# A two-layer decoder trunk on one core: where the reciprocal of the recurrence stands, how the first MLP marks its spare time, in what pieces a residual is loaded and which engine normalises

## The chip, the cores and the metric

The kernel runs on one core of a Trainium2 chip. A core has five engines that work side by side, each through its own list of instructions in order: TensorE (PE, the matrix multiplications and the transposes), VectorE (DVE, element-wise work on vectors), ScalarE (ACT, functions and casts), GpSimd (POOL) and SyncE (SP, which only issues transfers here). Transfers between the large memory and the core's own memory run on 16 DMA engines. An engine that reaches an instruction whose input is not there waits, and everything behind that instruction on the same engine waits with it.

The metric is the device time of one execution in microseconds (us). Before the change it was 2046.99 us, the median of 3 runs (2044.89 to 2050.0).

## What is computed

The trunk has two layers of width 1024 over 1024 positions, all in float32. Each layer is a mixer and an MLP, each followed by a layer norm of the scaled residual plus the branch:

```
for i in range(2):
    mix = hgrn2_mixer(x, ...)  if i == 0 else  conformer_conv_mixer(x, ...)
    x = layer_norm(ALPHA * x + mix, ...)
    ff = square(relu(x @ ffn_w1[i])) @ ffn_w2[i]        # 1024 -> 4096 -> 1024
    x = layer_norm(ALPHA * x + ff, ...)
```

The first mixer is a gated linear recurrence with 8 heads: projections of x give q, a forget gate, v and an output gate; per head a state `S` of 128 by 128 is carried along the sequence, `S_t = diag(f_t) S_{t-1} + k_t v_t^T` and `o_t = S_t^T q_t`; then a norm, a gate and an output projection. The second mixer is a convolution module: a projection to 2048 columns, a gate, a causal depthwise convolution over 31 positions, a layer norm with a sigmoid gate, and a projection back to 1024.

## The kernel before, in words

Every float32 product is made of reduced-precision products. A factor is split into a rounded high part and the rest (a cast on ACT, then a subtraction on DVE), and three matmuls take the place of one. On top of that the large products use a form with 7 instead of 8 block products, whose weight blocks are sums of blocks (`form`; `sum_pieces` and its relatives make these sums in the large memory by adding transfers). The unit of PE's work is a matmul of 128 by 128 by 512 columns, of which the kernel issues thousands in each stage.

The stages, by the time at which PE works on them in the profiled execution: the projection of v (5 to 85 us); the recurrence's heads with the other projections as filler (85 to 410); the output projection and norm (410 to 504); the first MLP's upward half (504 to 817) and downward half (817 to 1125); the first projection of the convolution in two halves of the sequence, with the convolution itself on DVE, ACT and POOL beside it (1125 to 1526); in that stretch the projection back, `second(0)` for the first half from about 1288 and `second(1)` for the other from about 1466; the second MLP (1526 to 2039). The last results leave by 2047.

Up to the end of the recurrence the order of the instructions is that in which the code was written. The heads are generators (from L700 on): each `yield` ends a step, a list of chores interleaves the steps with filler matmuls, and `later(1, ...)` defers a small job to the next step. After that a scheduler of the framework orders each engine's list by its own estimate of the times and by dependences; `keep_in_program_order` and `behind` restrict it.

What the change touches:

- **The recurrence's reciprocal.** For the part of the scores inside small blocks a head needs `kd`, on DVE the product of a cut of `B` with `rt`, the reciprocal of `totals[4]`. The reciprocal is issued one step ahead of that product (L730 to L733). `state` is the carried state: a copy and three updates, then three more updates, in two chains per head, and PE's products `state,qk` wait for them.
- **The spare work of the first MLP.** Weight blocks for the convolution's projections are split ahead of time and written back to the large memory under the names `ready`. `spare` (L1486) does one unit of it: a small DVE copy into `now` (a mark, which reads the form that PE takes next and so sets the earliest time), a cast on ACT and a subtraction on DVE of the block `next` loaded by the mark before, two stores of `ready`, and the load of the following `next`, held back by a small POOL copy that reads the mark. In the first MLP's upward half `Forms` calls it when a form is made, by the rate 3 in 8; there a POOL copy also holds back the cast (`late_cast`). In the downward half it is called 30 times. There are 38 units.
- **The gate of `sum_pieces`** (L453). The copies of a weight sum are held back by a transfer of one element, issued by SP from a form of the MLP.
- **The norm of the convolution**, `normalise`. For each half 8 pieces of 128 by 512 are scaled and shifted: 6 on ACT, 2 on DVE (the odd ones of the left columns).
- **The residual of `second(0)`**, `residual_of`. Four transfers of 512 KB bring it from `kept` into a buffer that the transposes of `finish` read before; they are issued after the last of its 8 column blocks.
- **The evictions of `second`** (from L1768). For each tile the product's result is added to the scaled residual, then a bias; for the right columns an operation named `ahead` scales the residual and adds the bias before the product is there.

Of the kernel before, what the change touches and what calls it, by code (L numbers as in the profile page):

```python
# [8 lines left out]
F32 = mybir.dt.float32  # L9
# [259 lines left out]
def body(ctx, tc, d, out):  # L269
# [24 lines left out]
    def run(kb, n, size):  # L294
        return [kb + i * size for i in range(n)]

    def slots(kbs, name):
        return ring(kbs, (2, 1024), name, F32R)

    def raws(kbs, name="raw"):  # L300
        return ring(kbs, (1024,), name)
# [153 lines left out]
    def sum_pieces(name, layer, c):  # L455

        t = sums[name, layer, c] = dram.tile([4, P, 1024], F32, name=f"sum_{name}{layer}{c}")
        v, w = t.rearrange("a p n -> p a n"), d[name][layer, c].rearrange("a p n -> p a n")

        def copy(i, q):  # L460
            def go(after):
                nc.sync.dma_start(out=t[i : i + 1, 0, 0:1], in_=after)
                nc.sync.dma_start(out=v[:, i], in_=w[:, q])

            return go

        def add(out, x, **kw):
            return lambda after: nc.gpsimd.dma_start(out=out, in_=x, accum_op=ALU.add, **kw)

        def chained(i):  # L470
            return add(v[:, i], v[:, i - 1], max_dma_last_dim=4096)

        return [copy(0, 0), copy(1, 2), add(v[:, 0:2], w[:, 2:4]), copy(2, 0), chained(2), copy(3, 1), chained(3)]
# [196 lines left out]
    def mul(o, a, b):  # L670
        vector.tensor_tensor(out=o, in0=a, in1=b, op=ALU.mult)

    def cutout(t, at, dims):
        return bass.AP(tensor=t.tensor, offset=t.offset + at, ap=[t.ap[0], *dims])
# [6 lines left out]
    def recurrence(h):  # L681
# [45 lines left out]
        yield  # L727
        rt, kd = p1("rt"), p1("kd")
        other, mine = [[n2 - 4, 2], [8, P], [1, 4]], [[n2 + 4, 2], [8, P], [1, 4]]
        vector.reciprocal(rt, totals[4])  # L730
        later(1, lambda: nc.scalar.copy(out=cutout(kd, 4, other), in_=cutout(B, 4, other)))
        yield
        mul(cutout(kd, 0, mine), cutout(B, 0, mine), cutout(rt, 0, [[1, 2], [2, P], [0, 4]]))  # L733
        scale(4)
        yield
# [747 lines left out]

    hold, staged = [], []

    def spare(after, late_cast=False):  # L1486

        if not hold:
            return
        slot, raw = hold  # L1490
        now = stat.tile([P, 2, 4], F32, tag="ss", name="ss")[:, 0, :1]
        nc.vector.tensor_copy(out=now, in_=after)
        if staged:
            key = staged.pop()
            if late_cast:
                nc.gpsimd.tensor_copy(out=slot[:, 0, :1], in_=now)
            nc.scalar.copy(out=slot[:, 0].bitcast(F32R), in_=raw)
            vector.tensor_tensor(out=slot[:, 1].bitcast(F32R), in0=raw, in1=slot[:, 0], op=ALU.subtract)
            ready[key] = tuple(dram.tile([P, 1024], F32, name=f"ready{len(ready)}_{i}") for i in range(2))
            for i in range(2):  # L1500
                nc.sync.dma_start(out=ready[key][i], in_=slot[:, i])
        if ahead:
            name, at = ahead.pop(0)
            nc.gpsimd.tensor_copy(out=raw[:, :1], in_=now)
            nc.sync.dma_start(out=raw, in_=d[name][at])
            staged.append((name, at))

    fw = Forms(nc, vector, slots((144, 152, 48, 112, 120), "fw"), raws(run(192, 4, 4)), raws(run(160, 2, 4), "sum"), lambda after: spare(after, True), 3, range(44))
    fw.todo = [[(blocks("w1q", 0, c), 2 if c < 2 else 0)] for c in range(NFC)]
    up = Up()  # L1510

# [7 lines left out]
    up.settle(0)  # L1519
    fw.ahead(3)  # L1520
    up.ws = bank((6, 7, 3, 4))
    summing = []
    for c in range(NFC):
        for i in ORDER[2 if c < 2 else 0 :]:
            (f,) = fw.take(1)
            fw.ahead(3)
            if (c, i) == (0, 7):
                bg.done()
            up.form(c, i, f)
            if summing:  # L1530
                summing.pop(0)(f[:1, 1, :1].bitcast(F32))
        if c in (0, 2):
            summing += sum_pieces(*to_sum.pop(0))
        if c == 0:
            up.settle(1)
            hold += [view(208, (2, 1024), F32, "spare"), view(216, (1024,), F32, "next")]
# [147 lines left out]
    def normalise(half):  # L1684

        for job in conv[KB * half : KB * half + KB]:
            bg.flush(job)
        while late:
            late.pop(0)()
        mv = stat.tile([P, NTB, 5], F32, tag="mv4", name="mv", bufs=2)  # L1690
        for t in range(NTB):
            vector.bn_aggr(mv[:, t, 0:2], cs[half][:, t])
        vector.tensor_scalar(out=mv[:, :, 2:3], in0=mv[:, :, 1:2], scalar1=LN_EPS, scalar2=None, op0=ALU.add)
        nc.gpsimd.tensor_tensor(out=mv[:, :, 3:4], in0=mv[:, :, 2:3], in1=nhalf[:, :NTB].rearrange("p (a b) -> p a b", b=1), op=ALU.pow)
        vector.scalar_tensor_tensor(out=mv[:, :, 4:5], in0=mv[:, :, 0:1], scalar=-1.0, in1=mv[:, :, 3:4], op0=ALU.mult, op1=ALU.mult)
        normed[0] = 1
        if half == 0:
            block_sums(*to_sum.pop(0), mv[:2, 0, 4:5])
        gate[1], gate[2] = [mv[:, 0, 4:5]] * 2, mv[:, 0, 4:5]
        for n in range(2):  # L1700
            for t in range(NTB):
                cv = ct[half][:, t, n * HT : (n + 1) * HT]
                if n == 0 and t % 2:
                    vector.tensor_scalar(out=cv, in0=cv, scalar1=mv[:, t, 3:4], scalar2=mv[:, t, 4:5], op0=ALU.mult, op1=ALU.add)
                else:
                    nc.scalar.activation(cv, cv, AF.Identity, bias=mv[:, t, 4:5], scale=mv[:, t, 3:4])

    def residual_of(half, y):
        for t in range(NTB):
            nc.sync.dma_start(out=y[:, t, :], in_=kept[half][t])  # L1710
        rest[half] = y

    rest, adds, gated = [None, None], [], {}
# [1 line left out]
    def finish(half):  # L1715

        st = sT[half]

        def one(j):
            pt = rings["aux"]()  # L1720
            for t in range(NTB):
                tensor.transpose(pt[:, t * P : (t + 1) * P], ct[half][:, t, j * P : (j + 1) * P], ident)
            z = big("z")
            sg = big("r")
            gj, bj = par[:, CLG + j : CLG + j + 1], par[:, CLB + j : CLB + j + 1]
            nc.scalar.activation(sg, pt, AF.Sigmoid, bias=bj, scale=gj)
            nc.scalar.activation(z, pt, AF.Identity, bias=bj, scale=gj)
            vector.tensor_tensor(out=z, in0=z, in1=sg, op=ALU.mult)
            gated[half] = split(st[:, 0, j, :], st[:, 1, j, :], z)
            if j == KB - 1 and half == 0:  # L1730
                residual_of(half, ct[0])

        bg.chores += [lambda j=j: (one(j), one(j + 1)) for j in range(0, KB, 2)]

    def second(half):
# [27 lines left out]
        for n, t in ((n, t) for n in range(2) for t in range(NTB)):  # L1763
            if t == 0:
                w = wa.take(4)
                wa.ahead(2)
            ps = acc()
            product(ps, wide(sT[half], t, w))  # L1768
            yv = y[:, t, n * HT : (n + 1) * HT]
            if n == 0 and (half == 1 or t < 2):  # L1770
                vector.scalar_tensor_tensor(out=yv, in0=yv, scalar=ALPHA, in1=ps, op0=ALU.mult, op1=ALU.add)
                vector.tensor_tensor(out=yv, in0=yv, in1=bp[:, :HT], op=ALU.add)
                yv = y[:, t, HT:]
                ahead = vector.scalar_tensor_tensor(out=yv, in0=yv, scalar=ALPHA, in1=bp[:, HT:], op0=ALU.mult, op1=ALU.add)
                if half == 1:
                    behind(ahead, gated[half])
            else:
                vector.tensor_tensor(out=yv, in0=yv, in1=ps, op=ALU.add)
            if n == 1:
                if half == 1:  # L1780
                    norm(y[:, t, :], g, b)
                    keep(half, t, y[:, t, :])
                    bg.chores.append(lambda t=t: back(t))
                    continue
                mu, rs = moments(y[:, t, :])
                off = stat.tile([P, 5], F32, tag="mv", name="mv")[:, 0:1]
                vector.scalar_tensor_tensor(out=off, in0=mu, scalar=-1.0, in1=rs, op0=ALU.mult, op1=ALU.mult)
                nc.scalar.activation(y[:, t, :], y[:, t, :], AF.Identity, bias=off, scale=rs)
                keep(half, t, y[:, t, :])
                bg.chores.append(lambda t=t: back(t))  # L1790
# [228 lines left out]
```

## Time and profile before

| | |
|---|---|
| median of 3 runs | 2046.99 us (2044.89 to 2050.0) |
| the profiled execution | 2048.95 us |
| its span in the trace | 2047.1 us |
| PE busy | 2021.1 us, 99% of the span, 11144 matmuls |
| DVE busy | 1489.3 us, 73% |
| ACT busy | 1094.0 us, 53% |
| POOL busy | 386.4 us, 19% |
| mean granted clock of PE | 0.999 |

The span is what the trace covers; 1.85 us of the execution lie outside. A row of a timeline gives the start, the duration, the engine, the line, the operation with what it writes and reads, how many are merged, and in brackets how long the engine sat idle before it and what released it. Matmuls overlap, so the duration of one is longer than the distance to the next, and idle time is shorter than the time lost between two starts. Most lines are those of helpers (L204, L72), so a row is known by the names of its tiles.

### The profile page before, as it was taken

Reading aid. Unit: us, or ns where it says so; the run is one execution under the profiler, and the core shown is the slowest. Engines: PE = TensorE matmul, PEld = TensorE weight load, DVE = VectorE, ACT = ScalarE, POOL = GpSimd, SP = SyncE. Lnnn points to the kernel's source line nnn. Section 1 sums busy time; section 2 is a strip of 40 time slices with the busy share of each in tenths; the row PEclk is TensorE's granted clock in tenths of the full one; section 3 lists DMA queues with packets and bytes.
Section 4 is the critical chain, followed back from the end, with each engine's and each line's share of the span. In section 5 each row is a group of like instructions: output and inputs, shape, how many; then the busy total and the mean of one; then the engine's idle time right before and its main releaser. Section 6 shows DMA issues by size and latency. Waiting matters only on the chain.

```text
span 2047.1 us, 29685 instructions
## 1 busy us (share of the span) xinstructions
PE 2021.1 (99%) x11144; PEld 1669.3 (82%) x11144; DVE 1489.3 (73%) x1978; ACT 1094.0 (53%) x1725; POOL 386.4 (19%) x403
## 2 busy tenths in 40 slices
PE   8999999999999999999999999999999999999998
PEld 7888887888787888888888888788888888888886
DVE  8698888877856676665667897889589676755456
ACT  5456566632655566444443776498625555443343
POOL 0113222111100000000001798089110000000002
PEclk9999999999999999999999999999999999999999
DMA  5779979742499876989998754797669788995542
GB/s 188 217 187 266 266 216 242 233 179 84 145 316 294 292 278 223 400 322 338 333 338 291 298 191 186 257 341 265 254 234 333 243 265 293 379 289 189 195 154 103
DMA packets 183124, 517.55 MB, mean 253 GB/s; under 512 B 17988, under 2 KB 49860, under 8 KB 181828
## 3 DMA queue, kind: packets, MB, share of 16 engines
q1 hardware_dynamic: 168036, 459.03, 62.3%
q0 software_dynamic: 14944, 56.63, 12.0%
q8 instruction: 87, 1.43, 0.3%
q14 instruction: 57, 0.47, 0.1%
HBM read 380.85 MB, written 201.85 MB: 285 GB/s over the span
## 4 chain that ended last, share of the span: by engine, by line
PE 79%; DVE 8%; DMA 6%; issue 3%; ACT 2%; POOL 2%; SPq 0%; DVEq 0%; POOLq 0%; ACTq 0%
PE ps L204 79%; POOL cb L204 1%; DMA next<-in_w1q_dram 1%; DMA dh<-hf 1%; DVE qk L204 1%; DMA ready<-spare 1%; DMA y<-kept 1%; DVE t L204 1%; DMA vr<-in_wv_dram 1%; DVE fs L204 1%; DMA next<-in_wpw_dram 1%; DVE xf L204 0%; DVE vr L204 0%; DVE spare L204 0%; DMA dr<-in_w_dram 0%
## 5 line engine op out<-in xcount | busy, mean ns | idle before, releaser
L204 PE MATMUL ps<-dw,dh 128*128 128x512 f32 x2688 | 611.1, 389 | 0.1
L204 PEld LDWEIGHTS ps<-dw,dh 128*128 128x128 f32 x2688 | 504.3, 188 | 104.8 <-ACT dh L72 0.5
L204 PE MATMUL ps<-x1f,fw 128*128 128x512 f32 x1344 | 307.5, 390 | 4.5 <-ACT fw L72 2.9
L204 PEld LDWEIGHTS ps<-x1f,fw 128*128 128x128 f32 x1344 | 251.5, 188 | 59.1 <-issue 2.7
L204 PE MATMUL ps<-xf,fs 128*128 128x512 f32 x1008 | 248.3, 397 | 0.8 <-DVE t L204 0.7
L204 POOL TENSOR_TENSOR cb<-cb,prod 128x512 f32<-128x512 f32 x168 | 223.0, 1335 | 12.6 <-ACT prod L1646 2.0
L204 PEld LDWEIGHTS ps<-xf,fs 128*128 128x128 f32 x1008 | 184.1, 188 | 39.3 <-DVE t L204 1.9
L204 DVE TENSOR_TENSOR dh<-dh 128x1024 fp32r<-128x1024 f32 x112 | 136.6, 1223 | 107.7 <-ACT dh L72 105.8
L204 DVE SCALAR_TENSOR_TENSOR ps<-u,par,ps 128x512 f32<-128x512 f32 x296 | 206.1, 750 | 11.0 <-ACT ps L1658 9.5
L204 PE MATMUL ps<-xa,wa 128*128 128x512 f32 x864 | 202.5, 392 | 0.8 <-DMA wa<-ready 0.7
L204 DVE TENSOR_TENSOR dw<-dr,dw 128x1024 fp32r<-128x1024 f32 x112 | 136.4, 1223 | 84.9 <-ACT dw L72 77.9
L72 ACT CAST dw<-dr 128x1024 fp32r<-128x1024 f32 x112 | 117.4, 1053 | 149.4 <-PE ps L204 128.9
L72 ACT CAST dh<-dh 128x1024 fp32r<-128x1024 f32 x112 | 117.3, 1050 | 137.2 <-DMA dh<-hf 136.7
L204 PEld LDWEIGHTS ps<-xa,wa 128*128 128x128 f32 x864 | 160.5, 188 | 34.4 <-DMA wa<-ready 1.1
L1646 ACT ACTIVATE prod<-u,par 128x512 f32<-128x512 f32 x168 | 119.8, 727 | 36.7 <-POOL cb L204 36.1
L565 POOL TENSOR_TENSOR mv<-mv,nhalf 128x1 f32<-128x1 f32 x32 | 42.2, 1319 | 374.4 <-DVE mv L204 364.0
L204 PE MATMUL ps<-xb,wa 128*128 128x512 f32 x384 | 91.1, 393 | 0.0
L204 PE MATMUL ps<-w,oT 128*128 128x512 f32 x384 | 89.8, 391 | 0.3 <-DVE oT L204 0.3
L204 PE MATMUL ps<-vw,xf 128*128 128x512 f32 x336 | 79.9, 400 | 5.8 <-ACT vw L482 5.1
L204 PEld LDWEIGHTS ps<-w,oT 128*128 128x128 f32 x384 | 71.5, 188 | 15.2 <-DVE oT L204 0.7
L204 PEld LDWEIGHTS ps<-xb,wa 128*128 128x128 f32 x384 | 71.1, 188 | 14.3
L204 PEld LDWEIGHTS ps<-vw,xf 128*128 128x128 f32 x336 | 64.6, 193 | 20.7 <-ACT vw L482 5.1
(255 smaller groups left out, 2875.6 us busy)
## 6 DMA issues: line engine op xcount, KB each, us to landing
wa<-ready SPq DMA_DIRECT2D x140, 512.0 KB, 5.0
dh<-hf SPq DMA_DIRECT2D x112, 512.0 KB, 4.9
sum_w<-in_w_dram POOLq DMA_DIRECT2D x38, 1024.0 KB, 10.1
ready<-spare SPq DMA_DIRECT2D x76, 512.0 KB, 5.0
raw<-in_w1q_dram SPq DMA_DIRECT2D x66, 512.0 KB, 4.5
dr<-sum_w SPq DMA_DIRECT2D x64, 512.0 KB, 6.1
hf<-ht SPq DMA_DIRECT2D x112, 256.0 KB, 5.4
dr<-in_w_dram SPq DMA_DIRECT2D x48, 512.0 KB, 5.0
```

The lines of the kernel that those rows point to most:

```text
L72: self.nc.scalar.copy(out=slot[:, 0, c], in_=raw[:, c])
L204: return op(*args, **kw)
L565: nc.gpsimd.tensor_tensor(out=dst, in0=src, in1=nhalf[:, :n], op=ALU.pow)
L1646: nc.scalar.activation(tp, u[:, k : k + HT], AF.Copy, scale=tap(j, k))
```

## The change

It has six parts. The reciprocal moves one step later, directly ahead of the product that uses it. In the first MLP, `Forms` no longer calls `spare`; the loop over the forms calls it at every third form taken from the second chunk on, 15 times in place of 13, without the POOL copy ahead of the cast and with the mark, the cast and the subtraction pinned in the order of the program. The gate of `sum_pieces` becomes a small DVE copy on which the transfer depends. `normalise` gives DVE two more pieces for the second half, so that both engines have four. The residual of `second(0)` comes in 8 transfers of 256 KB: the left 512 columns of the four tiles after the fourth column block, the right ones after the eighth. In `second(0)`, `ahead` is put behind the eviction of the same tile.

```
         def copy(i, q):
             def go(after):
-                nc.sync.dma_start(out=t[i : i + 1, 0, 0:1], in_=after)
-                nc.sync.dma_start(out=v[:, i], in_=w[:, q])
+                now = stat.tile([P, 2, 4], F32, tag="ss", name="ss")[:, 0, :1]
+                mark = tc.keep_in_program_order(nc.vector.tensor_copy(out=now, in_=after))
+                moved = nc.sync.dma_start(out=v[:, i], in_=w[:, q])
+                tc.add_manual_dep(moved.ins, mark.ins.name, mybir.DependencyInfo(mybir.DependencyClass.Sync, mybir.DependencyReason.DATA), reason="gate")
...
-        vector.reciprocal(rt, totals[4])
-        later(1, lambda: nc.scalar.copy(out=cutout(kd, 4, other), in_=cutout(B, 4, other)))
-        yield
+        later(1, lambda: nc.scalar.copy(out=cutout(kd, 4, other), in_=cutout(B, 4, other)))
+        yield
+        vector.reciprocal(rt, totals[4])
         mul(cutout(kd, 0, mine), cutout(B, 0, mine), cutout(rt, 0, [[1, 2], [2, P], [0, 4]]))
...
-    def spare(after, late_cast=False):
+    def spare(after, in_order=False):
...
+        pinned = tc.keep_in_program_order if in_order else lambda op: op
...
-            if late_cast:
-                nc.gpsimd.tensor_copy(out=slot[:, 0, :1], in_=now)
-            nc.scalar.copy(out=slot[:, 0].bitcast(F32R), in_=raw)
-            vector.tensor_tensor(out=slot[:, 1].bitcast(F32R), in0=raw, in1=slot[:, 0], op=ALU.subtract)
+            pinned(nc.scalar.copy(out=slot[:, 0].bitcast(F32R), in_=raw))
+            pinned(vector.tensor_tensor(out=slot[:, 1].bitcast(F32R), in0=raw, in1=slot[:, 0], op=ALU.subtract))
...
-    fw = Forms(nc, vector, slots(...), raws(...), raws(...), lambda after: spare(after, True), 3, range(44))
+    fw = Forms(nc, vector, slots(...), raws(...), raws(...))
...
             up.form(c, i, f)
+            if c:
+                formed[0] += 1
+                if formed[0] % 3 == 0:
+                    spare(f[:, 1, :1].bitcast(F32), True)
...
-                if n == 0 and t % 2:
+                if (half or n == 0) and t % 2:
...
-    def residual_of(half, y):
+    def residual_of(half, y, part=slice(D)):
         for t in range(NTB):
-            nc.sync.dma_start(out=y[:, t, :], in_=kept[half][t])
+            nc.sync.dma_start(out=y[:, t, part], in_=kept[half][t][:, part])
...
-            if j == KB - 1 and half == 0:
-                residual_of(half, ct[0])
+            if half == 0 and j % 4 == 3:
+                residual_of(half, ct[0], slice((j - 3) * P, (j + 1) * P))
...
-                vector.tensor_tensor(out=yv, in0=yv, in1=bp[:, :HT], op=ALU.add)
+                evicted = vector.tensor_tensor(out=yv, in0=yv, in1=bp[:, :HT], op=ALU.add)
...
-                if half == 1:
-                    behind(ahead, gated[half])
+                behind(ahead, gated[half] if half == 1 else evicted)
```

What this does to the lists of the engines is shown at three places. The first is DVE in the eighth head of the recurrence (head 7, counted from 0): `fs` is the subtraction that completes a split factor for PE's filler, `state` the carried state, `rt` the reciprocal and `kd` its product. Before:

```order
L204 COPY state<-ps 128x128
L204 SCALAR_TENSOR_TENSOR state<-state,dec,ps 128x128 x3
L204 RECIPROCAL rt<-f 128x256
L204 TENSOR_TENSOR fs<-pr,fs 128x512
L204 SCALAR_TENSOR_TENSOR state<-state,dec,ps 128x128 x3
L204 TENSOR_TENSOR kd<-qk,rt 128x2x128x4
```

The same place now:

```order
L204 COPY state<-ps 128x128
L204 SCALAR_TENSOR_TENSOR state<-state,dec,ps 128x128 x3
L204 TENSOR_TENSOR fs<-pr,fs 128x512
L204 SCALAR_TENSOR_TENSOR state<-state,dec,ps 128x128 x3
L204 RECIPROCAL rt<-f 128x256
L204 TENSOR_TENSOR kd<-qk,rt 128x2x128x4
```

The reciprocal has moved behind the second chain of state updates. In head 6 it moves from ahead of the first chain to behind it, with the second chain further on in both.

The second place is PE before the start of `second(1)`: `ident,cb` are the convolution's last transposes, `ident,y` those of the normalised columns, `xa,wa` the first projection that serves as filler, `wa,xb` the products of `second(1)`. Before:

```order
L204 MATMUL ps<-ident,cb 128x128 x4
L204 MATMUL ps<-xa,wa 128x512 x39
L204 MATMUL ps<-ident,y 128x128 x8
L204 MATMUL ps<-xa,wa 128x512 x12
L204 MATMUL ps<-ident,y 128x128 x8
L204 MATMUL ps<-wa,xb 128x512 x24
```

The same place now:

```order
L204 MATMUL ps<-ident,cb 128x128 x4
L204 MATMUL ps<-xa,wa 128x512 x44
L204 MATMUL ps<-ident,y 128x128 x16
L204 MATMUL ps<-wa,xb 128x512 x24
```

The 12 filler matmuls between the two groups of transposes are gone from there, and the last transposes of `cb` stand 7 matmuls closer to the end of the filler (44 against 39 and 12).

The third place is DVE at the first evictions of `second(0)`: `y<-y,ps` takes a product, `y<-y,b_pw` adds the bias (as SCALAR_TENSOR_TENSOR it is `ahead`), `ps<-u,par,ps` and `cb` belong to the convolution of the other half. Before:

```order
L204 SCALAR_TENSOR_TENSOR ps<-u,par,ps 128x512
L204 SCALAR_TENSOR_TENSOR y<-y,b_pw_10739 128x512
L204 SCALAR_TENSOR_TENSOR ps<-u,par,ps 128x512
L204 SCALAR_TENSOR_TENSOR y<-y,b_pw_10739 128x512
L204 TENSOR_TENSOR cb<-ps,cb 128x512
L204 SCALAR_TENSOR_TENSOR y<-y,ps 128x512 x2
L204 TENSOR_TENSOR y<-y,ps 128x512
L204 TENSOR_TENSOR y<-y,b_pw_10739 128x512 x2
```

The same place now:

```order
L204 SCALAR_TENSOR_TENSOR ps<-u,par,ps 128x512 x2
L204 TENSOR_TENSOR cb<-ps,cb 128x512
L204 SCALAR_TENSOR_TENSOR y<-y,ps 128x512 x2
L204 TENSOR_TENSOR y<-y,ps 128x512
L204 TENSOR_TENSOR y<-y,b_pw_10743 128x512
L204 SCALAR_TENSOR_TENSOR y<-y,b_pw_10743 128x512
L204 TENSOR_TENSOR y<-y,b_pw_10743 128x512
L204 SCALAR_TENSOR_TENSOR y<-y,b_pw_10743 128x512
```

Both `ahead` operations have moved from in front of the evictions to behind the ones of their tiles.

More of the change, by code (lines that the diff above doesn't have):

```diff
@@ L1490, in spare @@
         slot, raw = hold
+        pinned = tc.keep_in_program_order if in_order else lambda op: op
         now = stat.tile([P, 2, 4], F32, tag="ss", name="ss")[:, 0, :1]
-        nc.vector.tensor_copy(out=now, in_=after)
+        pinned(nc.vector.tensor_copy(out=now, in_=after))
         if staged:
             key = staged.pop()
-            if late_cast:
-                nc.gpsimd.tensor_copy(out=slot[:, 0, :1], in_=now)
-            nc.scalar.copy(out=slot[:, 0].bitcast(F32R), in_=raw)
-            vector.tensor_tensor(out=slot[:, 1].bitcast(F32R), in0=raw, in1=slot[:, 0], op=ALU.subtract)
+            pinned(nc.scalar.copy(out=slot[:, 0].bitcast(F32R), in_=raw))
+            pinned(vector.tensor_tensor(out=slot[:, 1].bitcast(F32R), in0=raw, in1=slot[:, 0], op=ALU.subtract))
             ready[key] = tuple(dram.tile([P, 1024], F32, name=f"ready{len(ready)}_{i}") for i in range(2))
@@ L1506, in spare @@
             staged.append((name, at))
-    fw = Forms(nc, vector, slots((144, 152, 48, 112, 120), "fw"), raws(run(192, 4, 4)), raws(run(160, 2, 4), "sum"), lambda after: spare(after, True), 3, range(44))
+    fw = Forms(nc, vector, slots((144, 152, 48, 112, 120), "fw"), raws(run(192, 4, 4)), raws(run(160, 2, 4), "sum"))
     fw.todo = [[(blocks("w1q", 0, c), 2 if c < 2 else 0)] for c in range(NFC)]
@@ L1521, in body @@
     up.ws = bank((6, 7, 3, 4))
-    summing = []
+    summing, formed = [], [0]
     for c in range(NFC):
@@ L1529, in body @@
             up.form(c, i, f)
+            if c:
+                formed[0] += 1
+                if formed[0] % 3 == 0:
+                    spare(f[:, 1, :1].bitcast(F32), True)
             if summing:
-                summing.pop(0)(f[:1, 1, :1].bitcast(F32))
+                summing.pop(0)(f[:, 1, :1].bitcast(F32))
         if c in (0, 2):
```

## The prediction

> **What bounds the kernel now.** I read the page first. These are its span and its first section:
>
> ```profile
> span 2047.1 us, 29685 instructions
> PE 2021.1 (99%) x11144; PEld 1669.3 (82%) x11144; DVE 1489.3 (73%) x1978; ACT 1094.0 (53%) x1725; POOL 386.4 (19%) x403
> ```
>
> PE has work in 99% of the span, so a change that leaves PE's work alone, as this one does, can only win or lose time where PE waits. Second came the table of stretches, for the price of a matmul that never waits and for the load of the DMA engines, and third PE's own waits (total, times, longest):
>
> ```profile
> 680.00:780.00 100.00, 100.00 (x443) 82.81 (x442) 69.56 (x82) 61.01 (x90) 4.62 (x11) 1.00 0.76 262
> 817.00:849.00 32.00, 32.00 (x143) 26.50 (x142) 16.50 (x20) 12.09 (x14) 2.96 (x9) 1.00 1.02 383
> 839.00:849.00 10.00, 10.00 (x46) 8.29 (x45) 3.91 (x5) 3.76 (x4) 0.00 (x0) 1.00 1.03 412
> ```
>
> ```profile
> PE ps L204 <- ACT fw L72: 2.9, 2, 1.5
> PE ps L204 <- DVE state L204: 1.6, 2, 1.3
> PE ps L204 <- ACT c L1318: 1.2, 1, 1.2
> ```
>
> A matmul of 512 columns costs 100/443 = 0.226 us; the clock column is 1.00 throughout. No wait is long: the change speaks to single stalls of about 1 us. So I went to each place in the timelines and asked what is late next when its stall goes.
>
> **The recurrence: the stall in head 6 comes back, head 7 pays.** From PE's timeline, then DVE's:
>
> ```profile
> 333.25 0.49 PE L204 MATMUL ps<-state,qk 128*128 128x128 f32 x2 [1.34 <-DVE state L204]
> ...
> 389.16 0.70 PE L204 MATMUL ps<-qk 128*32 128x32 f32 x32 [0.33 <-DVE blocks L204]
> ```
>
> ```profile
> 330.71 1.74 DVE L204 RECIPROCAL rt<-f 128x256 f32<-128x256 f32 x1
> ...
> 333.23 1.11 DVE L204 SCALAR_TENSOR_TENSOR state<-state,dec,ps 128x128 f32<-128x128 f32 x3
> ...
> 338.46 1.11 DVE L204 SCALAR_TENSOR_TENSOR state<-state,dec,ps 128x128 f32<-128x128 f32 x3
> ...
> 368.71 1.75 DVE L204 RECIPROCAL rt<-f 128x256 f32<-128x256 f32 x1
> 370.37 0.63 DVE L204 TENSOR_TENSOR fs<-pr,fs 128x512 fp32r<-128x512 f32 x1
> 371.48 1.11 DVE L204 SCALAR_TENSOR_TENSOR state<-state,dec,ps 128x128 f32<-128x128 f32 x3 [0.47 <-PE ps L204]
> 372.50 1.22 DVE L204 TENSOR_TENSOR kd<-qk,rt 128x1024 f32<-128x1024 f32 x1
> ...
> 388.67 0.43 DVE L204 COPY_PREDICATED blocks<-mask,ps 128x256 f32<-128x256 int32 x1
> ```
>
> In head 6 the reciprocal at 330.71 stands ahead of the first state chain, for which PE waits 1.34. Moved behind it, the chain starts 1.66 earlier (370.37 - 368.71 for the same instruction) and that wait goes. But none of the ten rows from 330.71 to 338.46 has an idle bracket: DVE works without a break, so the second chain at 338.46 comes at the same time whatever the order before it. PE, now 1.34 early, waits for that one instead. The price is 0; if the first wait's gain held, and the smaller one of that row too, it would be -1.6. In head 7 PE does not wait for the first chain. There DVE had a hole ahead of the second chain: it waits for PE at 371.48, with 0.47 idle, although the reciprocal filled part of the time. Now the reciprocal starts behind this chain, at about 372.50, and `kd` follows 1.66 later. None of the 28 rows from 372.50 to 388.67 has a bracket, so all of them move by 1.66, and the last is what PE waits for at 389.16. That wait has no slack left: +1.7 (bounds 0, if PE's own delay or an easier order absorbs it, and +2.2, the 1.66 with the 0.47 of the hole).
>
> **The first MLP: -0.4 and -1.2.** From ACT, SP and PE:
>
> ```profile
> 539.06 0.57 ACT L1318 COPY c<-ps 128x512 f32<-128x512 f32 x1
> 539.53 1.99 ACT L1094 CAST x1f<-x 128x1024 fp32r<-128x1024 f32 x2
> 541.43 1.05 ACT L72 CAST fw<-sum 128x1024 fp32r<-128x1024 f32 x1
> ...
> 651.70 1.05 ACT L1497 CAST spare<-next 128x1024 fp32r<-128x1024 f32 x1 [3.98 <-DMA next<-in_wpw_dram]
> ```
>
> ```profile
> 640.80 1.10 SPq L1505 DMA_DIRECT2D next<-in_wpw_dram  x1
> ```
>
> ```profile
> 653.29 6.89 PE L204 MATMUL ps<-x1f,fw 128*128 128x512 f32 x29 [1.18 <-ACT c L1318]
> ```
>
> PE waits for the cast at 541.43. The scheduler now puts a copy of `c`, which takes 539.53 - 539.06 = 0.47, behind such a cast instead of ahead: -0.4 (0 to -0.5). At 651.70 ACT stands 3.98 in front of the cast of a spare block whose load was issued at 640.80, 10.9 before; behind it is the copy of `c` that PE waits for. With a mark at every third form there are 3 x 24 x 0.226 = 16.3 us between marks, more than those 10.9, so the block is there: -1.2 for PE's 1.18. With the one-element gates SP loses a wait, and DVE gains 8 small copies that stand beside PE's work. Should a block be late again, it now is late in a list that may not be reordered, and the same stall stands once more: bounds -1.6 and +1.5.
>
> The end of this stage has two more units in it, since the last mark now lies near 795 (the 15th) and not at 746. By the stretches above, the DMA engines are full from 817 to 849 (share 1.02), and a block of 512 KB takes 524/412 = 1.27 us at the rate there. I take the two units as landed before 817, with +0.3 for a quarter of a block (-0.2 to +2).
>
> **The downward half's end: -0.7.**
>
> ```profile
> 1126.58 3.78 PE L204 MATMUL ps<-xa,wa 128*128 128x512 f32 x15 [0.69 <-DMA wa<-ready]
> ```
>
> ```profile
> 1115.55 1.58 SPq L1501 DMA_DIRECT2D ready<-spare  x2
> ...
> 1122.26 1.77 SPq L81 DMA_DIRECT2D wa<-ready  x4
> ```
>
> The loads at 1122.26 wait for the last stores of `ready` at 1115.55. Two marks more in the upward half let the staging end earlier, so that these stores leave the queue: -0.7 (-0.9 to 0).
>
> **`second(0)`: -0.6 and -1.0.**
>
> ```profile
> 1285.04 2.31 PE L204 MATMUL ps<-xb,wa 128*128 128x512 f32 x9
> ...
> 1287.94 0.66 PE L204 MATMUL ps<-ident,y 128*128 128x128 f32 x4 [0.16 <-ACT z L1727]
> ...
> 1289.93 1.66 PE L204 MATMUL ps<-wa,xa 128*128 128x512 f32 x6 [0.28 <-DVE xa L204]
> ...
> 1293.10 7.12 PE L204 MATMUL ps<-wa,xa 128*128 128x512 f32 x30 [0.17 <-ACT xa L1094]
> ...
> 1314.42 5.96 PE L204 MATMUL ps<-wa,xa 128*128 128x512 f32 x25 [1.03 <-DVE y L204]
> ```
>
> ```profile
> 1301.96 2.11 SPq L1710 DMA_DIRECT2D y<-kept  x4
> ```
>
> ```profile
> 1310.84 0.69 DVE L204 SCALAR_TENSOR_TENSOR y<-y,b_pw 128x512 f32<-128x512 f32 x1 [3.33 <-issue]
> ```
>
> 15 filler matmuls instead of 9 between the first groups of transposes are 6 x 0.226 = 1.4 us, more than the three idle times 0.16 + 0.28 + 0.17: -0.6 (-0.8 to 0). The evictions hang behind `ahead` at 1310.84, which stands 3.33 for a residual issued at 1301.96. The left columns are now issued four blocks sooner, and the evictions need them alone and stand ahead of `ahead`: -1.0 (-1.2 to +0.2, if smaller transfers land later).
>
> That last bound rests on how halved transfers fare. The page's last section has both sizes for one pair of tiles:
>
> ```profile
> hf<-ht SPq DMA_DIRECT2D x112, 256.0 KB, 5.4
> ...
> hf<-ht SPq DMA_DIRECT2D x8, 512.0 KB, 6.9
> ```
>
> 256 KB lands in 5.4 us where 512 KB takes 6.9, so the left halves gain by size as well as by their early issue. The Trainium skill, "DMA: Bandwidth & Descriptors", section "Measured (HBM→SBUF, 128 partitions, SWDGE, issued from GpSimd)", speaks against the edit: it says to batch transfers to 1 MiB or more, since smaller ones reach less of the peak. By its two figures, 0.95 us for 64 KB and 6.15 for 1 MB, the residual would occupy the engines about 2.4 us longer as eight pieces than as four, an estimate from that page, and the sum without this gain would be 1.0 higher.
>
> **`second(1)`: +1.7.**
>
> ```profile
> 1462.03 3.02 PE L204 MATMUL ps<-xa,wa 128*128 128x512 f32 x12
> ...
> 1466.21 5.74 PE L204 MATMUL ps<-wa,xb 128*128 128x512 f32 x24 [0.29 <-ACT xb L1094]
> ```
>
> ```profile
> 1462.36 0.77 ACT L1726 ACTIVATE r<-ps,par 128x512 f32<-128x512 f32 x1
> ```
>
> From the first sigmoid at 1462.36 to the first product at 1466.21 the chain (sigmoid, scale, product, cast) takes 3.85 us, and the 12 filler matmuls at 1462.03 covered 2.7 of it. In the new list of PE they stand ahead of all 16 transposes. Then only the second group of transposes, about 1.0, lies beside the chain: PE idles 2.85 less what ACT saves. ACT's two operations for `ha`, which stood inside the chain, come ahead of it, worth about 0.9: near 2.0 idle in place of 0.29, +1.7 (+0.5 if the chain starts after four transposes and runs unbroken, +2.5 if nothing of it is saved). That ACT does four pieces of the norm and not six does not help here: the columns are ready before PE has come through its filler.
>
> **The sum.** 0 + 1.7 - 0.4 - 1.2 + 0.3 - 0.7 - 0.6 - 1.0 + 1.7 = -0.2 against the profiled execution of 2048.95 us (span 2047.1, and 1.85 around it). That execution lies 1.96 above the median of the runs, so on the median's scale the forecast is 2046.99 - 0.2 = 2046.8 us. About 0.3%, 6.1 us, is what a measurement of this kernel can tell from no change.
>
> **Rivals.** (1) *Every gain holds and nothing is given back*: the order hides the reciprocal in head 7, and `xb` is early. With -1.6, 0, -0.5, -1.6, -0.2, -0.9, -0.8, -1.2 and +0.5 the sum is -6.3, 2040.7 us. For it speaks that each stall is really in the trace; against it the unbroken rows of DVE and the lost filler. (2) *Slower: the staging reaches the downward half's first loads.* The two added units bring six transfers of 512 KB. If they are still in the queues when the DMA engines are full, each sets the loads of PE's first blocks back by 1.27, together 7.6, and the forecast without its +0.3 becomes 2054.1 us. From the first such transfer on the kernel is slower than before, and by over 0.3% only with all six; against it, the mark near 795 has over 20 us until 817. (3) *The halved residual lands no sooner*: SP reaches the left loads only behind the `wa` loads, and the bound +0.2 holds for -1.0: 2048.0. The Trainium skill's rule on batches, named above, would act here. (4) *The marks do not do what they say*: a block takes longer than 16.3 us, and 0 stands for -1.2: 2048.0.
>
> Chances: forecast 0.60, (1) 0.15, (2) 0.05, (3) 0.10, (4) 0.10. Faster by over 0.3% means under 2040.9; two thirds of (1), and 0.02 of the forecast's low tail: 0.12. Slower means over 2053.1: 0.05, nearly all (2). The rest, 0.83, is no change. The range leaves out (2) and most of (1) and takes in the forecast's bounds as far as they can meet, with the 2 to 3 us that the runs shown lie from their median: 2041.5 to 2050.0.
>
> **What would show it.** Right: PE waits for `state` at the second chain of head 6, for about 1.3; its wait for `blocks` near 389 has grown to about 2; no `next` ahead of a cast near 650; no wait for `y` near 1313; about 2 idle ahead of `wa,xb` near 1466. Wrong: a wait for `dh` or `dw` near 849 of several us (2), no wait at all in heads 6 and 7 and at `second(1)` (1), or a time outside the range with these waits as said.

## The result and the profile after

The changed kernel takes 2051.05 us (median of 22 runs, 2049.15 to 2054.03) where the kernel before takes 2047.99 (22 runs of its own, 2044.89 to 2052.22): ratio 1.0015, 95% interval 1.001 to 1.0021. It is about 3 us slower, outside the range given and on the other side of no change. The difference is half of the 0.3% that one measurement can tell; many runs together tell it.

The profiled execution took 2050.17 us. These are the first lines of its page:

```profile
span 2048.4 us, 29679 instructions
PE 2018.4 (99%) x11144; PEld 1668.4 (81%) x11144; DVE 1494.1 (73%) x1990; ACT 1094.2 (53%) x1723; POOL 390.0 (19%) x391
```

The span is only 1.3 longer than before, since the execution profiled before lay 0.96 above its median of now and this one 0.88 below its own. The two traces are therefore compared place by place, and the runs decide on the sum. PE's waits after:

```profile
PE ps L204 <- DVE state L204: 4.0, 3, 1.7
PE ps L204 <- DVE t L204: 3.5, 3, 1.5
PE ps L204 <- ACT z L1732: 2.5, 2, 1.8
PE ps L204 <- ACT fw L72: 1.5, 1, 1.5
PE ps L204 <- ACT c L1320: 1.4, 1, 1.4
```

The waits for `state` rose from 1.6 to 4.0, and two new ones lead: `t` and `z`. The next table has PE alone by stretches (time, PE busy with its matmuls, clock, share of the DMA engines, GB/s), after:

```profile
85.00:180.00 95.00, 91.62 (x907) 1.00 0.82 217
340.00:410.00 70.00, 66.41 (x826) 1.00 0.75 212
600.00:700.00 100.00, 100.00 (x443) 1.00 0.90 295
1125.00:1288.00 163.00, 163.00 (x755) 1.00 0.59 212
1288.00:1340.00 52.00, 52.00 (x251) 1.00 0.84 276
1460.00:1530.00 70.00, 66.78 (x325) 1.00 0.63 224
```

And the same stretches before:

```profile
85.00:180.00 95.00, 94.26 (x924) 1.00 0.84 229
340.00:410.00 70.00, 69.22 (x838) 1.00 0.78 222
600.00:700.00 100.00, 98.74 (x435) 1.00 0.89 300
1125.00:1288.00 163.00, 162.14 (x751) 1.00 0.61 228
1288.00:1340.00 52.00, 50.52 (x237) 1.00 0.79 260
1460.00:1530.00 70.00, 68.89 (x332) 1.00 0.64 233
```

Three stretches are filled (600 to 700 and both from 1125 to 1340), and three have lost 2 to 3 us each: two in the recurrence and one at `second(1)`.

PE does the same 11144 matmuls in both kernels, and the same ones in the same order up to the first MLP. So a second reading is exact there, and off by the few matmuls that changed places further on: the start of PE's n-th matmul, after minus before. It is +0.69 at the 400th (the projection of v, which the change does not touch), +1.92 at the 600th, +3.43 at the 1000th, +3.89 at the 1800th, +2.15 at the 3000th, +3.79 at the 3200th and +5.61 at the 4000th, the end of the recurrence. Then it falls to +3.75 at the 5000th (first MLP), to -0.34 at the 8400th, and ends at +1.47 behind `second(1)`. The steps of +1.24, +1.43 and +1.82 in heads 0, 1 and 7 are one pattern. Head 0, DVE before:

```profile
116.07 1.75 DVE L204 RECIPROCAL rt<-f 128x256 f32<-128x256 f32 x1
117.73 0.63 DVE L204 TENSOR_TENSOR fs<-pr,fs 128x512 fp32r<-128x512 f32 x1
118.28 1.21 DVE L204 TENSOR_TENSOR kd<-qk,rt 128x1024 f32<-128x1024 f32 x1
...
120.67 0.68 DVE L204 SCALAR_TENSOR_TENSOR t<-t,ps 128x512 f32<-128x512 f32 x1
```

Head 0, DVE after:

```profile
117.81 0.69 DVE L204 TENSOR_TENSOR fs<-pr,fs 128x512 fp32r<-128x512 f32 x1 [0.97 <-ACT fs L663]
118.42 1.75 DVE L204 RECIPROCAL rt<-f 128x256 f32<-128x256 f32 x1
120.20 1.23 DVE L204 TENSOR_TENSOR kd<-qk,rt 128x1024 f32<-128x1024 f32 x1
...
122.60 0.68 DVE L204 SCALAR_TENSOR_TENSOR t<-t,ps 128x512 f32<-128x512 f32 x1
```

`fs` starts at 117.73 and at 117.81: in both it waits for ACT's cast. Before, the reciprocal filled that wait to the last tenth, and no row showed a wait. After, DVE stands idle for 0.97, does `fs`, and only then the reciprocal, so `t` comes 1.93 later. PE needs `t`, after:

```profile
123.33 1.65 PE L204 MATMUL ps<-xf,fs 128*128 128x512 f32 x6 [1.54 <-DVE t L204]
```

In head 1 the hole is a wait for PE and the victim is the second state chain. DVE before, where the copy of `state` stands behind the reciprocal (143.14 to 144.89) and has no bracket:

```profile
145.35 0.28 DVE L204 COPY state<-ps 128x128 f32<-128x128 f32 x1
```

DVE, then PE, after:

```profile
146.90 0.29 DVE L204 COPY state<-ps 128x128 f32<-128x128 f32 x1 [0.88 <-PE ps L204]
147.22 1.12 DVE L204 SCALAR_TENSOR_TENSOR state<-state,dec,ps 128x128 f32<-128x128 f32 x3
148.26 1.75 DVE L204 RECIPROCAL rt<-f 128x256 f32<-128x256 f32 x1
```

```profile
156.04 0.49 PE L204 MATMUL ps<-state,qk 128*128 128x128 f32 x2 [1.49 <-DVE state L204]
```

Head 6 went as written: its wait stands at the second chain now. In head 7 DVE is idle 2.10 ahead of its second chain, the hole that was written, but PE pays at `t` soon after; its wait for `blocks`, where the delay was forecast, stays as it was (0.32 against 0.33). PE after, then DVE:

```profile
342.62 0.49 PE L204 MATMUL ps<-state,qk 128*128 128x128 f32 x2 [1.72 <-DVE state L204]
...
381.25 3.02 PE L204 MATMUL ps<-xf,fs 128*128 128x512 f32 x12 [1.54 <-DVE t L204]
...
394.77 0.70 PE L204 MATMUL ps<-qk 128*32 128x32 f32 x32 [0.32 <-DVE blocks L204]
```

```profile
375.24 1.11 DVE L204 SCALAR_TENSOR_TENSOR state<-state,dec,ps 128x128 f32<-128x128 f32 x3 [2.10 <-PE ps L204]
376.26 1.75 DVE L204 RECIPROCAL rt<-f 128x256 f32<-128x256 f32 x1
```

### The profile page after: what moved, and what is told of

Same layout as the page of the kernel before. It is cut to its first block, busy times and chain, and to the rows that moved or that the text cites. A ratio compares the mean times of both kernels' runs of the same rounds, so it can differ in the third digit from the quotient of the medians.

```text
span 2048.4 us, 29679 instructions
## 1 busy us (share of the span) xinstructions
PE 2018.4 (99%) x11144; PEld 1668.4 (81%) x11144; DVE 1494.1 (73%) x1990; ACT 1094.2 (53%) x1723; POOL 390.0 (19%) x391
## 3 DMA queue, kind: packets, MB, share of 16 engines
q8 instruction: 87, 1.43, 0.3%
## 4 chain that ended last, share of the span: by engine, by line
PE 90%; DVE 6%; ACT 1%; issue 1%; DMA 1%; POOL 0%; SPq 0%; DVEq 0%; ACTq 0%; POOLq 0%
PE ps L204 90%; DVE qk L204 1%; DVE t L204 1%; DMA vr<-in_wv_dram 1%; DVE xf L204 1%; DVE fs L204 0%; DVE vr L204 0%; DVE rt L204 0%; DVE state L204 0%; DVE kd L204 0%; DVE pr L204 0%; DVE xr L204 0%; ACT x1f L1096 0%; DVE vw L204 0%; DVE f L204 0%
## 5 line engine op out<-in xcount | busy, mean ns | idle before, releaser
L1505 POOL COPY next<-ss 128x1 f32<-128x1 f32 x38 | 21.1, 554 | 423.6 <-DVE spare L204 367.6
L72 ACT CAST fw<-raw 128x1024 fp32r<-128x1024 f32 x56 | 58.8, 1050 | 47.7 <-PE ps L204 36.1
```

Of the source, the lines that this page charges most:

```text
L72: self.nc.scalar.copy(out=slot[:, 0, c], in_=raw[:, c])
```

## The experiments

Theory A: the move of the reciprocal is the loss. Where it had filled a wait of DVE, its 1.66 us now stand behind that wait (heads 0, 1, 7, a part of it in head 3), and the rest of the change gains. Theory B: the two profiled executions differ by themselves in the recurrence, and the loss comes from later stages. The runs below were timed in four groups, each beside runs of the kernel before, whose median lay between 2047.46 and 2048.72 in them; ratios are against it. The changed kernel was in none of the groups, so a difference to it is one between groups. "Early" is the reciprocal's old place, "late" its new one.

**The changed kernel with the reciprocal early.**

```
+        vector.reciprocal(rt, totals[4])
         later(1, lambda: nc.scalar.copy(out=cutout(kd, 4, other), in_=cutout(B, 4, other)))
         yield
-        vector.reciprocal(rt, totals[4])
```

> The changed kernel with one part undone: the reciprocal stands one step ahead of its product again, as before. Theory A (holes): moved behind a place where DVE waits anyway, the reciprocal no longer fills that wait, and its 1.66 us are added to everything behind it on DVE. By PE's positions in the two traces this costs 1.24 in head 0, 1.43 in head 1, 0.45 in head 3 and 1.84 in head 7, together about 5.0, and 0 in head 6. So this kernel is about 5 us faster than the changed one, near 2046.1, and 1.9 faster than before. Theory B (the later stages): the two profiled executions differ by themselves up to 410 us, and the loss is that of the second projection's second half; then this kernel stays within 1 us of the changed one, at 2050 to 2052.

2046.04 us, ratio 0.9984 (0.9975 to 0.9992): faster than before, and 5.0 faster than the changed kernel, or 5.7 when each is taken against the kernel before beside it. PE's waits:

```profile
PE ps L204 <- ACT z L1732: 2.5, 2, 1.8
PE ps L204 <- DVE state L204: 1.4, 2, 1.0
PE ps L204 <- DVE t L204: 0.7, 2, 0.4
```

`state` and `t` are back at what they were, and only `z`, which belongs to `second(1)`, is left of the new waits. From the 400th to the 4000th matmul PE's distance to before changes by -0.05 where the changed kernel had +4.92. Theory B is out.

**The kernel before with the reciprocal late, in all heads and in heads 0, 1 and 7.** The edit of the first is the hunk of the change; the second puts it under a condition, and the third has the other five heads.

```
+        late = h in (0, 1, 7)
+        if not late:
+            vector.reciprocal(rt, totals[4])
         later(1, lambda: nc.scalar.copy(out=cutout(kd, 4, other), in_=cutout(B, 4, other)))
         yield
+        if late:
+            vector.reciprocal(rt, totals[4])
```

> The kernel before with one part done: the reciprocal alone moves next to its product. Theory A: 5.0 slower than before, near 2053, with waits of PE for t or state of 1.2 to 1.8 in heads 0, 1 and 7, and one wait of about 1.7 in head 6, at its second chain and no longer at its first. Theory B: within 1 us of before.

> The kernel before, the reciprocal moved in heads 0, 1 and 7 alone, where DVE had a wait that it filled. Theory A: 1.24 + 1.43 + 1.84 = 4.5 slower than before, nearly all of what the move costs in all eight heads. Theory B, or a cost that is the same in every head: at most 3/8 of what the move of all eight costs, so under 2.

> The kernel before, the reciprocal moved in heads 2 to 6 alone, the five that have no wait of DVE behind the old place, or one that is given back. Theory A (holes): in the recurrence 0.45 in head 3 and 0 in the other four, although five of the eight reciprocals move; PE's wait of head 6 goes from the first chain to the second. Rival (each moved reciprocal costs the same): 5/8 of the move of all, about 3 in the recurrence. What the changed order does after the recurrence comes on top in both and is read from PE's positions apart from it.

| late in | ratio (95% interval) | median, us | recurrence (400th to 4000th matmul) | first MLP (4600th to 5600th) |
|---|---|---|---|---|
| all heads | 1.0038 (1.0026 to 1.0051) | 2056.70 | +5.44 | +4.06 |
| 0, 1, 7 | 1.0038 (1.0024 to 1.0052) | 2056.39 | +4.68 | +2.81 |
| 2 to 6 | 1.0018 (1.0009 to 1.0027) | 2051.89 | +0.32 | +4.01 |

The recurrence is as theory A has it: three heads cost 4.68 (4.5 expected), five cost 0.32 (0.45 expected), and a cost that is the same in every head would have been 1.9 and 3.1 of the 5.0. The steps come at the same matmuls in all three traces in which heads 0, 1 and 7 are late (the changed kernel and two here), with 1.2 to 1.3, 1.4 and 1.8. The places are what shows it, since one trace's total can mislead: of nine traces with the early reciprocal eight stay within -0.1 to +0.8 of before in the recurrence, and the ninth (the norm alone, below) is at +2.9, because PE waits 2.51 for `kt` in head 3 there. In the run with heads 2 to 6, head 6 shows the wait handed on: none at the first chain, and at the second

```profile
339.03 0.49 PE L204 MATMUL ps<-state,qk 128*128 128x128 f32 x2 [1.71 <-DVE state L204]
```

The totals are 3 to 4 above what was expected, and the last column says where: in the first MLP. There a scheduler writes the order, from its own estimate of the times; with the recurrence shifted it wrote another list for ACT, the same one in all three runs, and with the marks of the kernel before PE waits more often. Which change of that list does it was not followed. The run with all heads late has, in PE's timeline,

```profile
655.94 5.73 PE L204 MATMUL ps<-x1f,fw 128*128 128x512 f32 x24 [1.35 <-ACT c L1318]
663.09 2.11 PE L204 MATMUL ps<-x1f,fw 128*128 128x512 f32 x8 [1.42 <-ACT c L1318]
```

The changed kernel, with its new marks and gates, has nothing of the kind in the same stage.

**Marks and gates apart.** One run has the regular marks alone on the kernel before, one the gates alone, and one the gates with the residual in halves, whose first MLP is that of the gates alone. The edits are the hunks of the change.

> The kernel before with the regular marks of the first MLP and nothing else. Gains: the stalls of 1.34 and 0.24 near 650, 0.9 at the end of the downward half. In this list too the filler ahead of the second half is gone, 1.7 to 2.1. Together 0.3 to 0.9 faster or slower, which is the same as before; if the regular marks themselves cost time, slower by more than 1.

> The kernel before with the gates of the weight sums as small DVE copies and nothing else; marks irregular, with their POOL copies. Theory C (the gate is what the marks needed): the run with the regular marks alone stood 3.4 at 647, behind stores that SP issued late, since SP waits for the one-element transfer before it may issue the copy over it. Without that transfer SP runs on, and the stalls of 1.34 and 0.24 near 650 go: 1.5 faster than before. Rival (regular marks are the cure): the stalls near 650 stay, same as before within 0.5.

> The gates and the residual in halves, nothing else. The filler ahead of the second half is kept in this list. Against the gates alone it should gain the evictions' stall near 1313, 1.0 to 1.2, if the residual's late landing was its cause; if the operation ahead in front of the eviction is the cause, nothing, since it still stands there and now waits for the right half.

Marks alone: 2052.52, ratio 1.0025 (1.0014 to 1.0036). Gates alone: 2050.97, 1.0014 (1.0005 to 1.0023). Gates and halves: 2049.78, 1.0012 (1.0003 to 1.0021). Marks alone came out as the last clause has it (slower by more than 1); gates alone missed both cases; gates and halves lie 1.2 below gates alone, as their first case has it, but the two intervals overlap. From the 4600th to the 5600th matmul PE's distance to before changes by +3.81, +0.93 and +4.56, and by -1.89 in the changed kernel and in each of the four runs below and above that have both parts. Marks alone leave one wait of 3.26 and DVE standing for stores of `hf` that land late; PE and DVE:

```profile
650.58 9.79 PE L204 MATMUL ps<-x1f,fw 128*128 128x512 f32 x36 [3.26 <-ACT c L1318]
```

```profile
640.46 0.69 DVE L204 SCALAR_TENSOR_TENSOR ht<-ht,hr 128x512 f32<-128x512 f32 x1 [8.11 <-DMA hf<-ht]
```

Gates alone take the stall near 650 away, as expected, and give others; in the run with the halves PE and ACT show

```profile
690.11 10.10 PE L204 MATMUL ps<-x1f,fw 128*128 128x512 f32 x37 [4.39 <-ACT c L1320]
```

```profile
681.87 1.05 ACT L1499 CAST spare<-next 128x1024 fp32r<-128x1024 f32 x1 [10.12 <-DMA next<-in_wpw_dram]
```

ACT stands 10.12 in front of the cast of a block that has not landed: a mark of the old kind. In these traces each part alone has a stall in this stage, and the five with both parts have none from 600 us on. That each part alone exposes the other's stall is an inference; what makes the stores late with marks alone was not followed.

The first MLP is not the whole loss of either part. Gates alone lose 3.5 more at the start of the downward half, where PE waits near 853 (the run with the halves, the same code there, loses 0.4):

```profile
PE ps L204 <- ACT dh L72: 2.0, 1, 2.0
```

Marks alone lose 3.5 at `second(1)`: in their list, too, the filler is gone. With the old marks the same code also differs from run to run: gates alone and gates with halves are one code in this stage and changed by +0.93 and +4.56; the kernel before and the next two runs, again one code there, lost 1.9, 1.2 and nothing.

**The norm alone and `ahead` alone.** Each is one hunk of the change on the kernel before.

> The kernel before with four pieces of the norm on each engine and nothing else. In this list PE keeps its 12 filler matmuls between the two groups of transposes. If the lost filler is what costs 1.7 to 2.1 ahead of the second half's projection, this kernel is the same as before within 0.5. If the split of the norm costs it, 1.7 slower at that place.

> The kernel before with the operation ahead put behind the eviction and nothing else. In this list the 12 filler matmuls are gone, as in the changed kernel, though the norm is split as before. If the lost filler costs: 1.7 to 2.1 more ahead of the second half's projection, and the eviction's stall of 1.2 near 1313 stays, since the residual still comes late in one piece: 1 to 2 slower than before. If the norm's split costs: nothing there.

Norm alone: 2046.44, ratio 0.9997 (0.9988 to 1.0006). `ahead` alone: 2051.16, 1.0014 (1.0005 to 1.0023). PE at `second(1)`, norm alone:

```profile
1463.09 1.04 PE L204 MATMUL ps<-ident,y 128*128 128x128 f32 x8
1463.88 2.99 PE L204 MATMUL ps<-xa,wa 128*128 128x512 f32 x12
1466.71 1.24 PE L204 MATMUL ps<-ident,y 128*128 128x128 f32 x8
1467.79 5.75 PE L204 MATMUL ps<-wa,xb 128*128 128x512 f32 x24
```

And `ahead` alone:

```profile
1460.31 1.03 PE L204 MATMUL ps<-ident,y 128*128 128x128 f32 x8
1463.07 0.66 PE L204 MATMUL ps<-ident,y 128*128 128x128 f32 x4 [1.73 <-ACT z L1727]
1464.41 0.82 PE L204 MATMUL ps<-ident,y 128*128 128x128 f32 x4 [0.68 <-ACT z L1727]
```

The filler decides. `ahead` alone takes it away, and so do the marks alone; in the changed kernel with the reciprocal early it is still gone, and it is back when `ahead` is put back too (below), which shows the order of `ahead` as what takes it there. The norm's split, with the filler kept, even removes the 0.29 that stood there before. On the other half of the expectation `ahead` alone missed: the eviction's wait near 1313 is gone (PE runs 122 matmuls without a break from 1299.66), though the residual still came in one piece. That its median lies 3.6 above before while its trace ends within 0.3 is not explained; the trace had none of the first MLP's stalls near 650, which the other runs may have had.

The price of the lost filler differs from trace to trace: 1.8 in the changed kernel, 3.2 to 3.5 with the reciprocal early, with marks alone and with `ahead` alone. In those three the granted clock of PE drops to 0.50 for 3.41 us behind the wait (with the reciprocal early from 1461.7 to 1465.1), and matmuls of 512 columns start 0.427 apart and not 0.226. In the changed kernel's trace the clock stays at 1.00 there.

**Without the losing parts.** The change with the reciprocal early and without the order of `ahead`; the same without the norm's split; and the first with `ahead` put behind the eviction for the second tile alone:

```
                 if half == 1:
                     behind(ahead, gated[half])
+                elif t == 1:
+                    behind(ahead, evicted)
```

> The change without two parts: the reciprocal as before, and the operation named ahead in the first half's projection not put behind the eviction. In this list PE has its 12 filler matmuls back between the two groups of transposes ahead of the second half. Theory A with the filler: 1.9 faster than the changed kernel with its reciprocal as before, less up to 1.2 if the eviction's stall comes back: 2044.2 to 2045.4. If the four norm pieces on each engine, which this kernel keeps, are what delays the second half, it gains nothing there: near 2046.1 or above.

> The change without the moved reciprocal, without ahead behind the eviction and without the norm's split. The same as the run with these three parts and the norm's split (2043.84) within 0.5, since the split alone left every place unchanged: 2043.3 to 2044.4, 4 to 5 faster than before.

> The change with the reciprocal as before and ahead put behind the eviction for the second tile alone. In this list PE keeps the 12 filler matmuls ahead of the second half (37 and 12), and one of the two ahead operations still stands in front of the evictions. If the filler is worth its 1.8 here too, PE stands at the second half 5.5 to 6 ahead of before plus nothing lost there, so 4.5 to 6 faster than before by its trace, and 2042.5 to 2044 by the runs: the best of all. If the one ahead left in front still holds the evictions for the right half of the residual, a stall of 0.7 to 1.1 near 1309 remains and the time is that of the run without any ahead behind, 2043.8.

2043.84 us, ratio 0.9976 (0.9967 to 0.9985); 2044.92, 0.9986 (0.9977 to 0.9995); 2046.22, 0.9989 (0.998 to 0.9998). All three beat the kernel before, the first by 3 to 7 us by its interval, and the changed kernel by more. The first lies 0.4 below its range and the second 0.5 above; against the kernel before beside it the second is 2.5 faster, not 4 to 5. What the norm's split is worth therefore stays open, since the two intervals overlap. In the first, PE goes through `second(1)` without a wait:

```profile
1458.70 2.99 PE L204 MATMUL ps<-xa,wa 128*128 128x512 f32 x12
1461.53 1.24 PE L204 MATMUL ps<-ident,y 128*128 128x128 f32 x8
1462.61 5.76 PE L204 MATMUL ps<-wa,xb 128*128 128x512 f32 x24
```

The third did not become the best. It keeps its filler, but a wait near 1309 stays, as its second case had it, and PE loses 2.0 near 1360, where it waits for `u` and `xa`, against 1.0 in the first. Behind that wait its clock stands at 0.50 from 1362.2 to 1365.6, which costs another 1.6: 8 matmuls 0.2 late each. The scheduler moved something else; how the lists lead to that was not followed.

## Why the prediction was wrong, point by point

What failed is the part headed "The recurrence: the stall in head 6 comes back, head 7 pays". It priced two heads of eight, and put 0 on the others without saying so. Its own test for head 7 (is there a hole of DVE that the reciprocal filled?) was applied only where a bracket showed one. In heads 0 and 1 the reciprocal filled the hole wholly. It could have been read: before, ACT's two casts of `fs` in head 0 are the row

```profile
116.47 1.16 ACT L661 CAST fs<-pr 128x512 fp32r<-128x512 f32 x2
```

so the last ends at 117.63, and DVE's `fs` starts at 117.73 with or without a reciprocal ahead of it.

| term of the sum | forecast | measured, from the two traces |
|---|---|---|
| heads 0, 1, 3 | 0, unsaid | +1.24, +1.43, +0.45 |
| head 6 | 0 | 0 (-1.65, then +1.64) |
| head 7 | +1.7 | +1.82 |
| the copy of `c` behind the cast | -0.4 | 0: the wait for `fw` (1.42) became one for `c` (1.39) |
| marks and gates | -1.2 | -1.9 |
| start of the downward half | +0.3 | -0.4 |
| end of it, and `second(0)` | -2.3 | -3.7 |
| `second(1)` | +1.7 | +1.8 |

The table adds up to +0.8 (+0.7 by its rounded entries), and with +0.7 from the projection of v, which the change doesn't touch, to the +1.47 at PE's end. The two profiled executions differ by 1.22; that the one lay 0.96 above its median and the other 0.88 below adds the 1.84 that lead to the 3.06 of the medians. The three heads, 3.1, are the largest error. The gaining terms were right in mechanism, but for the copy of `c`, and together 2.4 too small; how much the marks and gates gain depends on which stalls the kernel before happened to have in the run that is compared. In head 7 the place was wrong, not the price: PE met the delay at `t`, 13.5 us ahead of `blocks`. Of the signs listed for being right, this one failed and the other four came.

For `second(1)` the forecast named the lost filler but not what had moved it; the norm's split, which it discussed, is not it. That its +1.7 meets +1.8 is in part luck: in the three other traces without the filler the place costs 3.2 to 3.5, by a drop of the clock that the forecast did not price. Of the rivals, none was this. The one on the slower side, staging in the way of the downward half's loads, did not occur in the changed kernel: PE's distance fell there.

For the residual the forecast also let the halves gain by size, from one pair of tiles (5.4 against 6.9; the second is a row of the full list of transfers, not of the page). They did not land sooner after their issue: the first left piece took 11.7 us where a whole one took 10.8 before. What can have helped is that it was issued at 1290.5 and not at 1302.0. The rule of the Trainium skill on batches ("DMA: Bandwidth & Descriptors", its section on measured bandwidth) was not put to a test by itself. The halves were in every run that beat the kernel before clearly, but `ahead` alone removed the eviction's wait without them, and with them, `ahead` not reordered, the eviction's wait still varied between nothing and 1.06 (the time lost between two starts of PE near 1309 to 1317). What the halves alone are worth stays open.

## What to carry to other kernels

An instruction on a busy engine may be filling a wait that no row shows. Before moving it, look up when the input of the next instruction arrives: if that is when the moved one ends, its place was free, and at the new place it costs time again unless there is a hole there too (1.24 to 1.82 us in three heads here, 0.45 in a fourth). A wait that is taken away on an engine without idle time can be handed to the next one, and where a scheduler orders the list, an edit in one stage reorders another, so each part has to be timed alone and with the others.

## What the runs showed that was not expected

Two parts that each cost time alone (2050.97 and 2052.52 us against 2047.5) gain together: five traces have -1.89 in the same stage, and the run with both, the halves and nothing else is 2.5 us faster than before (1 to 5 by its interval). The -1.89 is all that the trace before lost there; the old parts lost nothing in the trace of `ahead` alone. And one list of instructions is not one time: with the old marks the same code lost between 0 and 1.9 us in the first MLP of three traces, by when a transfer landed. A store of `hf` issued at 630.0 in the run with the marks alone landed 10.3 us later, where the page before has a median of 5.4 for its kind; but the kernel before has one of 11.0 itself (issued at 625.8).

A wait of PE can cost more than its bracket. In nine of the fourteen traces (not in the two of before and after) the granted clock drops to 0.50 for 3.41 us at or right behind a wait, once to three times; 7 or 8 matmuls that start 0.2 late each are 1.4 to 1.6 us. It is not the wait alone: PE waits 1.5 us for `fw` near 530 in all fourteen traces, and the clock drops behind it in five; there it costs nothing, since PE then waits for the next `fw` 1.2 less. What decides the drop was not followed.
